# A hybrid decoder block in split fp32: the first unit's steps, the place of the units' joins, copies of operands, and a stored product added by transfer

## The chip, the cores and the metric

The kernel runs on one core of a Trainium2 chip. The metric is device microseconds of one execution. The time before is 2474.84 us, the median of three runs (2473.66 to 2476.01).

## The reference, cut to what matters

One layer on a sequence of 256 tokens with 4096 channels, all in fp32: a norm, one wide projection that gives seven parts, two branches (a pooling mixer and a short gated convolution, 2048 channels each), a merge by sigmoid gates, an output product with a residual, and a last norm.

```python
h = rmsnorm(x, norm_w[l])
proj = jnp.einsum('bsd,de->bse', h, w_in[l])
u_p, z_p, u_c, b_c, c_c, z_c, g_logit = jnp.split(proj, SPLIT_POINTS, axis=-1)
y_pool = causal_multiscale_pool(u_p, pool_w[l], pool_scale[l]) * jax.nn.silu(z_p)
y_conv = causal_gated_shortconv(u_c, b_c, c_c, conv_w[l], conv_b[l]) * jax.nn.silu(z_c)
ys = jnp.stack([y_pool, y_conv], axis=2)
br = jnp.einsum('bsnc,ncd->bsnd', ys, w_branch[l])
gates = jax.nn.sigmoid(g_logit.reshape(b, s, N_BRANCHES, d) + gate_b[l])
merged = jnp.sum(gates * br, axis=2)
x = x + jnp.einsum('bsd,de->bse', merged, w_out[l])
...
return rmsnorm(x, final_norm_w)
```

`causal_gated_shortconv` is `b_gate * (conv_b + taps over 3 tokens of (c_gate * u))`. `causal_multiscale_pool` is a trailing mean over 2, 4, 8 or 16 tokens less the token itself, times a 512 x 512 matrix for each of four groups.

## The kernel before, in words

**Split operands.** Each fp32 operand of a product is split into a high part (rounded to the type fp32r by ScalarE, `highs`, line 181) and a low part (the rest, by a subtraction on VectorE, `lows`, line 185). A product is three matmuls: high by high, high by low, low by high. Activations are the stationary operand (128 x 128, held split in `arena`), weights move (128 x 512, split in a ring of 15 cells, `ring`).

**Units.** The work is 32 units, each 256 tokens by 1024 output columns: for each half c of the convolution channels `cz`, `cb`, `cu`, `cc` (z, b, u and c parts of the projection); `pz`, `pu` for each half of the pooling channels; eight gate units `g0_c`, `g1_c`; eight branch units `b0_c` (pooling) and `b1_c` (convolution); four output units `o0` to `o3`. Their order is that of lines 702 to 714. A unit is a text of steps, one letter each; a step takes 256 input channels and a weight block of 1 MB (256 x 1024). **P** is a direct step: 8 products, 24 matmuls. **S** is a turned step: seven products in place of eight (21 matmuls), by the scheme of Strassen, with four sums of weight quarters on VectorE into the tile `parts` (lines 231 to 245) and four sums in the operand (`sums_s`, line 623). The x operands are 8 of kind P (4 blocks of 128 x 128, high and low) and 8 of kind S: six with 7 blocks and two with 8. An S operand of 8 blocks can also serve a direct step (`standing`, line 149). The first unit, cz0, has the text SIX5, `PPPPPSPSPSPSPSPS`; most others have EIGHT, `PSPSPSPSPSPSPSPS`; branch units have 8 steps (B0, B1).

**End of a unit.** Products collect in four PSUM banks E (direct sums) and, for S steps, four banks F (corners), which the transposes also use. When a bank has its last product, `evacuate` (line 341) copies an E bank by ScalarE into the tile E or Y, and `copy_corners` (line 347) an F bank into a slot of the raw ring, as soon as that slot (`Join`) has been given out. Behind the unit's last step `combine` (line 352) joins them on VectorE: two sums of 512, one subtraction of 1024, and two multiply-adds of 1024 by 1/rms (in the units of w_in) or one sum of 2048. Then the unit's epilogue is put on `queue`, from which each tick (six matmuls) pops one item (lines 888 to 893): `gap(n)` is n empty items. So `cb` has, after one empty item, E = E * Y (z times b), four empty ones and then 16 transposes in four items (line 386), whose results ScalarE copies into Y; a store to DRAM follows. `cc` does the same, with the taps of the convolution behind the transposes. `b0_c` multiplies by its gates (Y = E * Y) and stores the product to `p_d`; `b1_c` multiplies, loads `p_d` back into Y, adds it on VectorE ten items later, transposes and stores `m_d`.

**Preparation.** Weights come as 1 MB loads on SyncE's queue into a raw ring of three slots; a slot is loaded anew when its step has been prepared (`pump`, line 862). A deque `work` holds, step by step, the items that split the weights. An item is issued when its step is within `state["limit"]`, which `after_group` sets to four steps beyond the current one (line 918), and when ring cells are free. The order in which the program issues instructions is pinned, and each engine runs its own in that order. So on VectorE and ScalarE what stands ahead of a join is what `pump` had issued before `combine` is called. `issue_load` gives a unit's Join its raw slot after the first three loads of the next unit (line 831).

**x operands.** They are made during cz0. `xc` blocks come on SyncE's queue into the tile Y; `x_direct` makes a P operand (ScalarE scales by the norm weight, VectorE does the low part); for an S operand `x_scale`, `x_sums` and `x_rest` work through two staging tiles, sa and sa2, over three steps' items (lines 811 to 817). In the same unit the squares of x are taken (`fetch_rows`, `square`), and 1/rms from them (`root`, before step 14).

**y and m operands.** From the last gate unit (g1_3) on, regions of the arena whose x operand has been used for the last time are filled with y operands (from `y_d`), later with m operands (from `m_d`, or for the last four straight from Y, `fill_direct`). A `Fill` is fetched by a transfer on GpSimd's queue into sa or a second tile sb, and six ticks or more later `fill_staged` makes it: four sums on VectorE, a rounding on ScalarE, a subtraction on VectorE (`parts_of`, line 629).

**Lines that the profile names.** 52 is any ScalarE activation, 55 any two-input sum or product on VectorE, 67 a multiply-add, 70 a load on SyncE's queue, 73 and 76 a plain and an adding transfer on GpSimd's queue, 386 the transposes, 900 the products, 524 a copy in the band tables, 1029 the last scaling of the output.

## Time and profile before

| | |
|---|---|
| runs, median of three | 2474.84 us (2473.66 to 2476.01) |
| the profiled execution | 2475.68 us |
| its span in the profile | 2473.9 us |
| TensorE products / weight loads | 2390.4 us (97%) / 1964.9 us (79%), 10497 instructions each |
| VectorE | 2155.7 us (87%), 1769 instructions |
| ScalarE | 1445.6 us (58%), 1401 instructions |
| GpSimd | 86.3 us (3%) |
| bytes moved | 553.36 MB, mean 224 GB/s |

How to read it. The span runs from the first to the last record of the profile; the execution's own time is 1.8 us more. A busy share is a mean over the whole span and says little here, since TensorE's is 97% and matmuls are counted busy while they wait in its pipeline. What counts is the chain of work that ended last, what ends each of TensorE's idle times, and how long a unit takes beside the time that its matmuls need in a stretch without a wait. In a row of the trace the columns are the start in us, the busy time, the engine, the line, the operation with output and inputs, and in brackets the idle time of the engine just before with what ended it. In a table of windows each row is a stretch of the span, its length, TensorE's busy time with its instructions, the granted clock, the share of DMA and GB/s. VectorE is written DVE, ScalarE ACT, GpSimd POOL, SyncE SP.

### The profile page before, as it was taken

What the parts mean: (1) busy time and instruction counts of PE and PEld (TensorE: products, weight loads), DVE (VectorE), ACT (ScalarE), POOL (GpSimd) and SP (SyncE); (2) the same over time, 40 slices, a digit from 0 to 9 for tenths busy, and PEclk for the clock granted to TensorE, in tenths of its full rate; (3) what the DMA queues carried; (4) which work ended last, traced back from release to release, by engine and by line L of the source; (5) the groups of instructions that cost most, each with busy time, mean ns of one, the idle gap of its engine ahead of it and who ended that gap; (6) DMA issues with size and microseconds to landing.
All of it is one profiled execution on the core that took longest, in us unless ns stands there. A gap on an engine that the chain in (4) does not pass through costs nothing.

```text
span 2473.9 us, 26884 instructions
## 1 busy us (share of the span) xinstructions
PE 2390.4 (97%) x10497; PEld 1964.9 (79%) x10497; DVE 2155.7 (87%) x1769; ACT 1445.6 (58%) x1401; POOL 86.3 (3%) x150
## 2 busy tenths in 40 slices
PE   8898999998999999999999999999899999999998
PEld 7577887887878888888888888887688887778886
DVE  7897899888889878978988998888888888889998
ACT  6665555654655655655665666565565555566664
POOL 0000000000000000000000000001000001000000
PEclk9999999999999999999999999999999999999999
DMA  8464565555556555555765776577667767647667
GB/s 323 154 233 177 187 220 208 192 199 200 194 209 215 199 190 205 208 204 202 249 228 192 260 244 232 194 252 255 233 238 265 269 249 261 231 178 267 239 219 271
DMA packets 83215, 553.36 MB, mean 224 GB/s; under 512 B 9488, under 2 KB 9488, under 8 KB 21008
## 3 DMA queue, kind: packets, MB, share of 16 engines
q1 hardware_dynamic: 68832, 484.47, 54.0%
q0 software_dynamic: 13824, 66.07, 8.8%
q8 instruction: 82, 1.34, 0.2%
q10 hardware_dynamic: 432, 1.11, 0.1%
q14 instruction: 45, 0.37, 0.0%
HBM read 522.25 MB, written 29.36 MB: 223 GB/s over the span
## 4 chain that ended last, share of the span: by engine, by line
PE 82%; DVE 10%; ACT 4%; issue 2%; DMA 2%; SPq 0%; DVEq 0%; POOL 0%; ACTq 0%; POOLq 0%
PE sums L900 61%; PE shared L900 19%; DVE ring L55 4%; ACT ring L52 3%; DVE parts L55 2%; PE shared L560 1%; PE shared L386 1%; DVE raw L55 1%; DMA raw<-in_w_in_dram 1%; DVE E L55 1%; DVE sa L55 1%; DVE arena L55 1%; ACT raw L52 0%; DVE E L67 0%; ACT E L52 0%
## 5 line engine op out<-in xcount | busy, mean ns | idle before, releaser
L900 PE MATMUL sums<-ring,arena 128*128 128x512 f32 x7827 | 1841.1, 393 | 33.6 <-ACT E L52 14.3
L900 PEld LDWEIGHTS sums<-ring,arena 128*128 128x128 f32 x7827 | 1477.5, 189 | 351.9 <-DVE ring L55 18.8
L55 DVE TENSOR_TENSOR ring<-raw,ring 128x2048 fp32r<-128x2048 f32 (+3 forms) x518 | 935.0, 1815 | 190.9 <-ACT ring L52 190.2
L52 ACT ACTIVATE ring<-raw 128x2048 fp32r<-128x2048 f32 (+3 forms) x518 | 787.6, 1535 | 436.5 <-PE sums L900 264.3
L52 ACT ACTIVATE ring<-parts 128x1024 fp32r<-128x1024 f32 (+1 forms) x418 | 412.6, 1002 | 330.6 <-DVE parts L55 296.1
L900 PE MATMUL shared<-ring,arena 128*128 128x512 f32 x2340 | 568.9, 392 | 9.6 <-DVE ring L55 7.3
L900 PEld LDWEIGHTS shared<-ring,arena 128*128 128x128 f32 x2340 | 440.4, 189 | 106.2 <-DVE ring L55 11.7
L55 DVE TENSOR_TENSOR ring<-parts,ring 128x2048 fp32r<-128x2048 f32 (+3 forms) x233 | 449.2, 1940 | 55.6 <-ACT ring L52 55.0
L55 DVE TENSOR_TENSOR parts<-parts,raw 128x512 f32<-128x512 f32 x390 | 270.2, 693 | 13.3
L55 DVE TENSOR_TENSOR parts<-raw 128x1024 f32<-128x1024 f32 x195 | 238.0, 1221 | 3.8 <-DMA raw<-in_w_branch_dram 2.3
L55 DVE TENSOR_TENSOR raw<-raw 128x512 f32<-128x512 f32 (+1 forms) x93 | 80.6, 867 | 2.1
L52 ACT ACTIVATE raw<-shared 128x512 f32<-128x512 f32 x124 | 67.7, 610 | 7.8 <-DVE ring L55 7.3
L52 ACT ACTIVATE arena<-sa 128x512 fp32r<-128x512 f32 (+2 forms) x28 | 22.1, 790 | 73.2 <-DVE sa L55 69.3
L52 ACT ACTIVATE E<-sums,rin 128x512 f32<-128x512 f32 x56 | 36.0, 686 | 25.8 <-PE sums L900 25.8
L386 PE MATMUL shared<-ident,E 128*128 128x128 f32 x128 | 20.8, 301 | 25.9 <-DVE E L55 25.9
L386 PEld LDWEIGHTS shared<-ident,E 128*128 128x128 f32 x128 | 17.0, 156 | 30.8 <-issue 27.4
L67 DVE SCALAR_TENSOR_TENSOR E<-raw,rin,E 128x1024 f32<-128x1024 f32 x28 | 34.7, 1282 | 0.6
L55 DVE TENSOR_TENSOR E<-E,Y 128x2048 f32<-128x2048 f32 x15 | 34.3, 2286 | 0.1
L52 ACT ACTIVATE Y<-shared 128x512 f32<-128x512 f32 x24 | 13.4, 596 | 32.7 <-PE shared L386 30.2
L55 DVE TENSOR_TENSOR arena<-sa,arena 128x512 fp32r<-128x512 f32 (+2 forms) x28 | 24.9, 888 | 8.7 <-ACT arena L52 8.7
L52 ACT ACTIVATE E<-sums 128x512 f32<-128x512 f32 x44 | 25.1, 595 | 11.6 <-PE sums L900 10.4
L76 POOL DMA_DIRECT2D E<-in_rows_dram x16 | 13.9, 867 | 441.8 <-DVE E L67 439.6
(108 smaller groups left out, 428.5 us busy)
## 6 DMA issues: line engine op xcount, KB each, us to landing
raw<-in_w_in_dram SPq DMA_DIRECT2D x319, 1024.0 KB, 4.8
raw<-in_w_branch_dram SPq DMA_DIRECT2D x64, 1024.0 KB, 5.7
raw<-in_w_out_dram SPq DMA_DIRECT2D x64, 1024.0 KB, 4.9
E<-in_rows_dram POOLq DMA_DIRECT2D x16, 512.0 KB, 10.0
gates_d<-E POOLq DMA_DIRECT2D x8, 1024.0 KB, 6.6
Y<-gates_d POOLq DMA_DIRECT2D x8, 1024.0 KB, 6.5
Y<-in_xc_dram SPq DMA_DIRECT2D x16, 256.0 KB, 6.1
E<-in_x_dram POOLq DMA_DIRECT2D x4, 1024.0 KB, 6.4
```

Of the source, the lines that this page charges most:

```text
L52: return pin(nc.scalar.activation(dst, src, func, **kw))
L55: return pin(nc.vector.tensor_tensor(out=dst, in0=a, in1=b, op=op))
L67: return pin(nc.vector.scalar_tensor_tensor(out=dst, in0=a, scalar=s, in1=b, op0=op0, op1=op1, **kw))
L76: return pin(nc.gpsimd.dma_start(dst, src, accum_op=ALU.add))
L386: pin(nc.tensor.transpose(shared(j)[:, i * T + t * P:i * T + (t + 1) * P], src[:, t, c:c + P], ident))
L560: pin(nc.tensor.matmul(o, a, b, start=(k, i) == (0, 0), stop=(k, i) == (3, 2)))
L900: pin(nc.tensor.matmul(ps, lhs, rhs, start=n == 0, stop=n == u.total[b] - 1))
```

## The change

- **First unit.** cz0 gets an order of its own, `FIRST`, in which all 16 steps are direct. Operands 8 to 15 are the S operands; six of them have no eighth block, which a direct step needs, so a tile `extra` holds it while the opening's pool is open (now for the first 10 steps). sa2 is gone: all eight S operands are staged through sa, and the sums, high and low parts come in one item. The tile `parts` is allocated when the opening's pool closes. A unit without S steps gets no Join, and `combine` does no join for it.
- **Joins.** A unit may have an `urgent` function, called at the end of `combine`. `cb`, `cc` and `b1` have E = E * Y there, `b0` Y = E * Y and its store; `pu` has an empty one. For a unit that has one, `after_group` sets the limit of preparation, during its last step, to two steps beyond the current one in place of four. The empty items in the epilogues are adjusted, so that the transposes of cb and cc come after six, those of b1 after fifteen.
- **Copies.** High parts of S operands, of those filled directly and of the x operands too, are made by `tensor_copy` on VectorE. P operands keep ScalarE. `fill_direct` stages in sa.
- **p0.** In `b1` the load of `p_d` into Y and the sum on VectorE go; two adding transfers on GpSimd's queue, one for each half of the tokens (512 KB), add `p_d` to E.

```diff
+FIRST = (0, 8, 9, 1, 10, 11, 2, 12, 13, 3, 14, 15, 4, 5, 6, 7)
+OPENED = 10
...
-    sums = sb("parts", [P, 4, NH])
...
+    extra = op.tile([P, NS, 2, P], F32R, name="extra")
...
-            assert i < self.n
+            if i == self.n:
+                e = extra[:, self.region[1]]
+                return e[:, 0], e[:, 1]
...
     def combine(u):
         d = u.dst
-        copy_corners(u)
...
-        u.join.prepared = True
+        if u.s:
+            copy_corners(u)
...
+            u.join.prepared = True
         u.flags["base"] = True
+        if u.urgent:
+            u.urgent()
...
-            return gap(1) + [lambda: mul(E, E, Y)] + gap(4) + transposes(E, copy) + [lambda: move(g_d[c], Y)]
+            return gap(6) + transposes(E, copy) + [lambda: move(g_d[c], Y)]
...
-            items = gap(1) + [lambda: mul(E, E, Y)] + gap(4)
+            items = gap(6)
...
+        in_unit(f"cz{c}", base + 3 * HALF, lambda u: silu_y(), FIRST if first else SIX4, dst=Y)
+        in_unit(f"cb{c}", base + HALF, b_epi, EIGHT).urgent = lambda: mul(E, E, Y)
...
+        in_unit(f"cc{c}", base + 2 * HALF, c_epi, EIGHT).urgent = lambda: mul(E, E, Y)
...
+        in_unit(f"pu{c}", c * NU, lambda u: [], EIGHT).urgent = lambda: None
...
-                return gap(2) + [lambda: mul(Y, E, Y), lambda: move(p_d[c], Y)]
+                return []
...
-            return gap(1) + [lambda: mul(E, E, Y), lambda: move(Y, p_d[c])] + gap(9) + [
-                lambda: add(E, E, Y)] + gap(5) + pairs(transposes(E, copy)) + [
+            return gap(15) + pairs(transposes(E, copy)) + [
...
+        def urgent():
+            if n == 0:
+                mul(Y, E, Y)
+                move(p_d[c], Y)
+            else:
+                mul(E, E, Y)
+                for t in range(2):
+                    gather(E[:, t], p_d[c][:, t])
...
+    def copy(dst, src):
+        return pin(nc.vector.tensor_copy(dst, src))
+
     def fill_staged(o, st):
         if o.kind == "S":
             sums_s(st)
-            parts_of(o, st[:, 0:o.n])
+            copy(o.view[:, 0], st[:, 0:o.n])
+            sub(o.view[:, 1], st[:, 0:o.n], o.view[:, 0].bitcast(F32))
...
-                if part == 0:
-                    act(o.view[:, 0, lo:hi], q)
-                else:
-                    sub(o.view[:, 1, lo:hi], q, o.view[:, 0, lo:hi].bitcast(F32))
+            copy(o.view[:, 0, lo:hi], q)
+            sub(o.view[:, 1, lo:hi], q, o.view[:, 0, lo:hi].bitcast(F32))
...
     def x_sums(j):
-        o, st = x_ops[first_order[j]], x_stage(j)
-        sums_s(st)
-        act(o.view[:, 0], st[:, 0:o.n])
...
+        o = x_ops[first_order[j]]
+        fill_staged(o, sa)
+        if o.n == 7:
+            e = extra[:, o.region[1]]
+            copy(e[:, 0], sa[:, A21])
+            sub(e[:, 1], sa[:, A21], e[:, 0].bitcast(F32))
...
-            steps[j].mid.append(item(x_rest, j))
...
-        loaded += mine[:3] + ([units[v - 1].join] if v else []) + mine[3:]
+        loaded += mine[:3] + ([units[v - 1].join] if v and units[v - 1].s else []) + mine[3:]
...
         state["limit"] = state["now"] + min(AHEAD, state["now"] + 1)
+        if u.urgent and st is u.steps[-1]:
+            state["limit"] = state["now"] + 2
...
-        if u is units[1]:
-            opening.close()
...
+            if state["now"] == OPENED:
+                opening.close()
+                sums = ctx.enter_context(tc.tile_pool(name="parts", bufs=1)).tile([P, 4, NH], F32, name="parts")
```

More of the change, by code (lines that the diff above doesn't have):

```diff
@@ L311, in __init__ @@
             self.flags = {}
+            self.urgent = None
             self.pending = deque()
@@ L353, in combine @@
         d = u.dst
-        copy_corners(u)
-        assert not u.pending
-        q = u.join.slot
-        add(q[:, 0], q[:, 2], q[:, 0])
-        add(q[:, 3], q[:, 0], q[:, 3])
-        sub(q[:, 0:2], q[:, 1:2].to_broadcast([P, 2, NH]), q[:, 0::3])
-        q = q.rearrange("p (n t) c -> p t n c", n=2)
-        d4 = d.rearrange("p t (n c) -> p t n c", n=2)
-        if u.scaled:
-            for t in range(2):
-                stt(d4[:, t], q[:, t], rin[:, t:t + 1], d4[:, t], ALU.mult, ALU.add)
-        else:
-            add(d4, d4, q)
-        u.join.prepared = True
+        if u.s:
+            copy_corners(u)
+            assert not u.pending
+            q = u.join.slot
+            add(q[:, 0], q[:, 2], q[:, 0])
+            add(q[:, 3], q[:, 0], q[:, 3])
+            sub(q[:, 0:2], q[:, 1:2].to_broadcast([P, 2, NH]), q[:, 0::3])
+            q = q.rearrange("p (n t) c -> p t n c", n=2)
+            d4 = d.rearrange("p t (n c) -> p t n c", n=2)
+            if u.scaled:
+                for t in range(2):
+                    stt(d4[:, t], q[:, t], rin[:, t:t + 1], d4[:, t], ALU.mult, ALU.add)
+            else:
+                add(d4, d4, q)
+            u.join.prepared = True
         u.flags["base"] = True
+        if u.urgent:
+            u.urgent()
     def corners(d):
@@ L430, in seq_x @@
     def seq_x(text):
+        if text is FIRST:
+            return [("P", i) for i in FIRST]
         return sequence(text, ND, ND + NS + NB, NB)
@@ L599, in branch_unit @@
                  before=lambda: move(Y, gates_d[n, c]))
+        u.urgent = urgent
         units.append(u)
@@ L647, in fill_direct @@
         add(st[:, Q3], k1[:, 0], st[:, Q6])
-        for part in (0, 1):
-            for lo, hi, q in ((0, 4, st[:, 0:4]), (A12, A11, k1), (A11, o.n, k0[:, 0:o.n - A11])):
-                if part == 0:
-                    act(o.view[:, 0, lo:hi], q)
-                else:
-                    sub(o.view[:, 1, lo:hi], q, o.view[:, 0, lo:hi].bitcast(F32))
+        for lo, hi, q in ((0, 4, st[:, 0:4]), (A12, A11, k1), (A11, o.n, k0[:, 0:o.n - A11])):
+            copy(o.view[:, 0, lo:hi], q)
+            sub(o.view[:, 1, lo:hi], q, o.view[:, 0, lo:hi].bitcast(F32))
         o.ready = True
@@ L763, in square @@
         stt(q[:, 1], q[:, 1], 1.0, q[:, 1], ALU.mult, ALU.mult, accum_out=ssq[:, 1, c:c + 1])
-    first_order = [i for _, i in seq_x(SIX5)]
+    first_order = FIRST
     xt = Y.rearrange("p a n -> p (a n)").rearrange("p (s o c) -> p s o c", s=4, c=P)
```

25 lines of the change are left out of this document (8 added, 17 removed).

## The prediction

> **What bounds the kernel now.** I read the clock first, then the chain that ended last, then what TensorE waited for, then unit by unit how far TensorE is from its own pace.
>
> ```profile
> core 0: 2473.9 us, clock 0.985
> ```
> ```profile
> PE 82%; DVE 10%; ACT 4%; issue 2%; DMA 2%; SPq 0%; DVEq 0%; POOL 0%; ACTq 0%; POOLq 0%
> ```
> ```profile
> PE shared L386 <- DVE E L55: 25.9, 5, 8.0
> PE sums L900 <- ACT E L52: 14.3, 2, 10.2
> ```
>
> TensorE ends the chain for 82% of the span. Its waits are few and long: 25.9 us before transposes (line 386) for VectorE's product in E, and 14.3 us in two places for ScalarE's copy of finished sums. The pace comes from a stretch without a wait, the first row here; the second is the transposes' wait:
>
> ```profile
> 198.19 9.68 PE L900 MATMUL sums<-ring,arena 128*128 128x512 f32 x42
> 215.14 1.09 PE L386 MATMUL shared<-ident,E 128*128 128x128 f32 x4 [7.26 <-DVE E L55]
> ```
>
> 42 products take 9.68 us with the drain of the last one (about 0.4), so 0.227 us each: 5.44 a direct step (24), 4.76 an S step (21). At that pace a unit of 360, 363 or 366 products takes 81.7, 82.3 or 83.0 us. Against that stand the stretches of the units concerned (length, TensorE's busy time, granted clock): cz0, cb0, cu0, cz1, cu1, pz0, g1_3, b1_3, o0.
>
> ```profile
> 7.14:114.60 107.46, 93.59 (x366) 0.95 0.65 249
> 114.60:198.20 83.60, 82.08 (x362) 1.00 0.57 202
> 198.20:292.30 94.10, 86.84 (x381) 0.95 0.53 190
> 374.40:467.90 93.50, 87.84 (x383) 0.96 0.58 204
> 549.70:644.50 94.80, 86.84 (x381) 0.95 0.52 193
> 726.30:818.90 92.60, 87.72 (x383) 0.96 0.57 206
> 1671.50:1769.40 97.90, 85.37 (x367) 0.97 0.71 242
> 2070.90:2124.10 53.20, 44.34 (x184) 0.97 0.70 245
> 2124.10:2216.80 92.70, 88.72 (x383) 0.96 0.55 199
> ```
>
> Over the pace they stand by 24.5, 1.9, 11.8, 10.5, 12.5, 9.6, 14.9, 11.7 (of 41.5 for 183 products) and 9.7 us: 107 us in all, part of it a clock granted at half for some us after a wait (0.95 to 0.97). That is what the change can reach.
>
> **A. The first unit (cz0).** Six S steps become direct: 18 products more, +4.1 us of TensorE, and VectorE and ScalarE lose the six weight sums. But eight of the x operands are needed earlier, each with its sums on VectorE, through one buffer sa.
>
> The start is later. ScalarE's order puts the scaling of the second operand (in steps[0].pre) ahead of the rounding of the first weights.
>
> ```profile
> 7.54 1.06 ACT L52 ACTIVATE ring<-raw 128x1024 fp32r<-128x1024 f32 x1 [0.46 <-DMA raw<-in_w_in_dram]
> 9.69 0.91 ACT L52 ACTIVATE arena<-Y,par 128x256 fp32r<-128x256 f32 x2 [1.09 <-DMA Y<-in_xc_dram]
> ```
>
> The second operand lands at 9.7, its scaling ends at 10.6, the first rounded half is there at 11.7: the first product moves from 7.14 to 11.7. Then one S operand's share of VectorE:
>
> ```profile
> 26.99 2.29 DVE L55 TENSOR_TENSOR ring<-raw,ring 128x2048 fp32r<-128x2048 f32 x1 [1.52 <-ACT ring L52]
> 29.20 1.01 DVE L55 TENSOR_TENSOR sa<-sa 128x128 f32<-128x128 f32 x4
> ...
> 34.38 1.09 DVE L55 TENSOR_TENSOR arena<-sa,arena 128x896 fp32r<-128x896 f32 x1
> ```
> ```profile
> L524 DVE CAST bands<-sa x4: 211/215/215, 320.4 to 1037.5; 128x128 fp32r<-128x128 f32 x4
> ```
> ```profile
> L1029 DVE TENSOR_SCALAR raw<-raw,rout x4: 747/751/754, 2458.5 to 2466.0; 128x1024 f32<-128x1024 f32 x4
> ```
>
> The 896-wide copy is not in the trace. It lies between the 128-wide copy, 0.21, and the two-input subtraction of its own width, 1.09; on the line between the one-input rows (0.21 at 128, 0.75 at 1024) it is 0.67, which I take. An operand costs 1.01 + 0.67 + 1.09 + 0.5 for the extra block = 3.3 us. With one buffer the next scaling (0.9) waits for that, the rounding of the step's weights (two of 1.06) stands behind it on ScalarE, and VectorE's lows (2.29) behind that: 8.6 us for an S operand after an S operand, against 5.44 for the step. Two of three operands are of that kind. From 10.6: lows of step 0 until 14.0, operand 8 until 17.2, scaling and rounding until 20.1, lows until 22.3. So step 1 starts at about 22 (17.4 before). A round S, S, P then takes VectorE's chain 17.4 us, or 18.7 with a square, and TensorE 3 x 5.44 = 16.3. VectorE leads by about 2 us after each direct operand, so I count 2 us of waits: 22.3 + 15 x 5.44 + 2 = 106 for the end of cz0, 114.6 before. In cb0 VectorE's lag goes (83.60 less 82.08, 1.5 us). The start of cu0 moves from 198.2 to 188: **-10.5**. Bounds: -14 (no waits at all) and -3 (each copy at 1.09, the chain late from the first round on).
>
> **B. Four turns (cb0, cc0, cb1, cc1).** VectorE now runs the next units' S step ahead of the join:
>
> ```profile
> 203.22 1.22 DVE L55 TENSOR_TENSOR parts<-raw 128x1024 f32<-128x1024 f32 x1 [1.05 <-DMA raw<-in_w_in_dram]
> ...
> 207.48 2.67 DVE L55 TENSOR_TENSOR raw<-raw 128x512 f32<-128x512 f32 x3
> 210.19 2.48 DVE L67 SCALAR_TENSOR_TENSOR E<-raw,rin,E 128x1024 f32<-128x1024 f32 x2
> 212.70 2.29 DVE L55 TENSOR_TENSOR E<-E,Y 128x2048 f32<-128x2048 f32 x1
> ```
>
> ```profile
> 198.68 2.04 ACT L52 ACTIVATE ring<-raw 128x1024 fp32r<-128x1024 f32 x2
> 200.58 1.12 ACT L52 ACTIVATE raw<-shared 128x512 f32<-128x512 f32 x2
> ```
>
> The unit ended at T = 198.2, the join began 9.3 us later and took 7.5 with the product. Its last two corner copies stood behind a weight rounding and ended at 201.7. In the changed order only the lows of two steps, both done near T, are ahead of the join on VectorE, and the four corner copies (0.56 each) stand together on ScalarE, the last right after T: join from T+0.9, product done at T+8.4. TensorE asks for it after 42 products, T+9.5. So nothing waits. What is late next is the third step's lows: T+8.4 + 2.3 = T+10.7, needed at 48 products and one set of transposes, about T+11.5. Of the 44.4 us over the pace in these four units, 25.0 are the wait (25.9 less 0.9 in b0_3); I keep 2.4 each for 16 transposes, and the other 9.8 are the half clock after the wait (the clock column, 0.04 to 0.05 of each stretch, allows up to 17, part of it inside the wait). **-35**; bounds -37 and -17 (half the wait stays as a wait for lows).
>
> **C. Staged S operands on VectorE (g1_3 to b0_0).** ScalarE stands before an operand's rounding, with the finished sums behind it:
>
> ```profile
> 1767.85 0.95 ACT L52 ACTIVATE arena<-sb 128x896 fp32r<-128x896 f32 x1 [3.29 <-DVE sb L55]
> 1768.70 1.83 ACT L52 ACTIVATE E<-sums,rin 128x512 f32<-128x512 f32 x3
> ```
>
> That rounding goes to VectorE, where 0.67 takes the place of a wait of 1.02. The sums are then copied at about T+5.5, after a P operand's rounding (that stays on ScalarE) and a weight rounding: the wait of 10.2 becomes 5.5. With a little less lag before it: **-5.5** (bounds -9, -1).
>
> **D. b0 to b1, the new wait.** The product and the join now stand ahead of the third step's lows:
>
> ```profile
> 1814.31 2.29 DVE L55 TENSOR_TENSOR ring<-parts,ring 128x2048 fp32r<-128x2048 f32 x1 [2.06 <-ACT ring L52]
> ...
> 1819.34 2.67 DVE L55 TENSOR_TENSOR raw<-raw 128x512 f32<-128x512 f32 x3
> 1822.05 2.29 DVE L55 TENSOR_TENSOR E<-E,raw 128x2048 f32<-128x2048 f32 x1
> 1824.37 2.29 DVE L55 TENSOR_TENSOR Y<-E,Y 128x2048 f32<-128x2048 f32 x1
> ```
>
> ```profile
> 1813.62 6.96 PE L900 MATMUL sums<-ring,arena 128*128 128x512 f32 x30
> ```
>
> b1_0 begins at T = 1813.6. The S step's lows end at T+3.0, join +5.0, product +2.2, third lows +2.3: T+12.5. TensorE needs them after 45 products, T+10.3. Behind them stand the fourth step's lows, which then come in time. Three turns of 2.1: **+6.5** (bounds 0 and +13, if half clock follows each).
>
> A rule bears on that. The Trainium skill, "TensorE: Matmul & The Clock Gate", section "What's actually happening", has the clock fall to half only after an idle window of about 3.4 us; by it these waits cost 6.3 alone. The trace agrees in that cb0 kept 1.00 through a wait of 1.5.
>
> **E. p0 by adding transfers (b1 to b0, o0).** One load and one sum on VectorE (2.29, beside TensorE) go; two adding transfers of 512 KB come, as in the out units:
>
> ```profile
> DMA to landing us min/median/max: 7.8/10.2/12.6
> ```
>
> They are issued after the product: join from T+0.9, 5.0 long, product 2.2, T+8.2. The longest landing, 12.6, ends at T+20.8 and the time between the two issues; the transposes come after 16 ticks of 6 products, T+21.8. It fits by less than 1: **+1**; bounds 0 and +8 (2 us late in each of four). Behind them POOL holds the stores after the transposes and loads of operands that are needed a unit later.
>
> The Trainium skill, "SBUF — State Buffer", section "Who interferes with whom", says that VectorE copies in a two-port mode shut GpSimd out while they run, descriptor writing included. By it a transfer issued beside a staged copy lands up to 0.7 later, and the sum would be +2; no row here shows it.
>
> **F. b1_3 and o0.** ScalarE waits here too:
>
> ```profile
> 2085.34 0.95 ACT L52 ACTIVATE arena<-sa 128x896 fp32r<-128x896 f32 x1 [10.54 <-DVE sa L55]
> ```
>
> That goes, and with it the wait for sums at o0's start (4.0). But in b1_3 the third lows stand behind the S step's lows (T+3.0), an S operand (2.6), the join (5.0), the product (2.2) and a P operand's subtraction (0.6), and take 2.2: T+15.6, needed at T+10.3. That is a wait of 5.3 and 1.6 of half clock (now 0.97 of 53.2): 41.5 + 6.9 = 48.4, 53.2 before. In o0 the four direct fills, about 2.9 us each with their copies, stand ahead of the lows of steps 7 and 8: some 2.5 us of waits and 1 for E's late transfer, 89 (92.7). **-8.5** (bounds -13, -1).
>
> **Sum.** -10.5 - 35 - 5.5 + 6.5 + 1 - 8.5 = -52. The profiled execution took 2475.68 (span 2473.9 and 1.8 around it), 0.84 over the median of the three: 2475.7 - 52 = **2424**. All low ends give 2403, all high ends 2475.
>
> **Rivals.** (1) *The cap starves VectorE's lead, slower than before.* If the join can't begin at T+0.9 but only when it does now, T+9.3, the two-step cap keeps the third lows behind it until T+19: 7.5 us of new wait and 1.6 of clock at seven branch turns, +64 in the place of D's 6.5, and B's gain turned into +6: about 2522. To undo 52 us at eleven turns it takes 4.7 each, so it decides from a join at about T+6. For it: the join starts at T+9.3 now. Against it: all that stands ahead of it there is named in the rows of B, and is behind it in the new order. (2) *The opening gains nothing*: the 8.6 us chain holds every step; A is 0, 2434. (3) *The branch waits are larger*: each third step and each E some 3 us later with the clock's half, +20, 2444. (4) *The change does half of what it says at the turns*: VectorE arrives later than its order suggests, B is -17, 2442. (5) *Better*: no waits in D, A and F at their low ends, 2409.
>
> **How the numbers follow.** The forecast has 0.45; (5) 0.12, (2) 0.11, (3) 0.12, (4) 0.10, (1) 0.08; 0.02 for failures that add up to no change. All but (1) and those 0.02 end well below 2470, where 0.2% (5 us, about what a measurement of this kernel can tell from no change) begins: faster 0.90, same 0.02, slower 0.08. The range 2402 to 2452 holds these but for their tails, and leaves out about 0.18.
>
> **What would show it.** First product near 11.7, cz0's end near 106. The waits for E at line 386 fall from 25.9 to under 5, while waits of TensorE for ring appear at the third step of b1 units (2 each, 5 in b1_3). ScalarE shows no wait for sa or sb beyond the first unit's end. I am wrong if cu0 starts after 195, if the first row of waits stays above 12, or if the branch units b0_0 to b1_2 take over 320 us (now 1769.4 to 2070.9, 301.5; with D and E about 309).

## The result, and the profile after

The changed kernel takes 2464.19 us (median of five, 2460.64 to 2464.99) against 2476.01 us for the kernel before (median of five): a ratio of 0.9951, 95% interval 0.9937 to 0.9966. It is faster by 0.5%, about 12 us. The prediction was 2424, faster by 52.

The profiled execution took 2464.99 us, its span 2463.3, 10.6 less than before. The first views are of the same kinds as those before the change: span and clock, the chain that ended last, and TensorE's waits (total us, times, longest).

```profile
core 0: 2463.3 us, clock 0.989
```
```profile
PE 77%; DVE 12%; DMA 4%; ACT 4%; issue 3%; DVEq 0%; SPq 0%; ACTq 0%; POOL 0%; POOLq 0%
```
```profile
PE sums L913 <- DVE ring L57: 25.2, 15, 7.0
PE shared L913 <- DVE ring L57: 9.8, 4, 6.0
PE sums L913 <- ACT ring L54: 9.8, 3, 7.8
PE shared L913 <- DVE Y L69: 8.7, 4, 2.5
PE sums L913 <- ACT E L54: 4.5, 1, 4.5
...
PE shared L394 <- DVE E L57: 0.7, 2, 0.4
```

The line numbers have moved: 54 is ScalarE's activation, 57 VectorE's two-input operation, 69 its multiply-add, 72 SyncE's load, 75 and 78 GpSimd's transfers, 394 the transposes, 913 the products (in the experiments some differ by a few). The wait that the change aims at has gone: the transposes' wait for E fell from 25.9 us to 0.7. Two others stand in its place: products that wait for VectorE's weight parts (25.2 and 9.8 us), and products that wait for the convolution's taps (8.7, `DVE Y L69`). DMA has risen from 2% to 4% of the chain.

The stretches, as a table of windows (length, TensorE busy, then the other engines, the granted clock, DMA share, GB/s): cz0, cu0, cz1, cu1, pz0, g1_3, the seven units b0_0 to b0_3 (b1_0 to b1_2 among them), b1_3, o0.

```profile
12.87:108.40 95.53, 92.04 (x385) 74.49 (x386) 79.78 (x115) 53.21 (x64) 2.14 (x3) 0.98 0.74 276
...
190.00:274.10 84.10, 84.10 (x380) 69.69 (x379) 75.32 (x60) 50.09 (x50) 5.27 (x23) 1.00 0.60 217
356.10:448.50 92.40, 88.06 (x383) 71.39 (x381) 80.20 (x72) 49.94 (x52) 2.05 (x3) 0.96 0.58 206
530.30:614.90 84.60, 84.30 (x380) 69.61 (x379) 75.16 (x57) 50.14 (x48) 0.55 (x1) 1.00 0.58 212
696.50:788.90 92.40, 87.33 (x383) 71.02 (x382) 80.07 (x69) 49.64 (x50) 2.01 (x3) 0.98 0.57 206
1641.40:1733.80 92.40, 84.57 (x368) 68.18 (x366) 80.11 (x76) 52.51 (x52) 9.29 (x16) 1.00 0.71 240
1733.80:2052.30 318.50, 307.58 (x1341) 252.06 (x1342) 253.50 (x186) 170.42 (x172) 22.43 (x34) 0.98 0.71 248
2052.30:2107.20 54.90, 46.06 (x184) 37.04 (x183) 47.76 (x53) 26.41 (x31) 3.75 (x7) 0.91 0.67 237
2107.20:2206.00 98.80, 88.30 (x383) 71.60 (x383) 84.94 (x94) 46.98 (x45) 2.31 (x3) 0.97 0.55 187
```

The seven branch units took this before:

```profile
1769.40:2070.90 301.50, 300.95 (x1342) 248.95 (x1343) 258.02 (x184) 175.45 (x176) 18.63 (x31) 0.99 0.71 257
```

So the gain and the loss stand in different places. cu0 starts 8.2 us earlier than before (190.0 for 198.2); cu0 and cu1 take 84 for 94; g1_3 takes 92.4 for 97.9. But cz1 and pz0 hardly moved, the branch units lost 17, b1_3 and o0 together 7.8 (153.7 for 145.9).

**Why the branch units lost.** One turn shows it, from b1_1 to b0_2, at 1912.8. VectorE, on its timeline:

```profile
1914.12 2.68 DVE L57 TENSOR_TENSOR raw<-raw 128x512 f32<-128x512 f32 x3 [1.12 <-ACT raw L54]
1916.84 2.29 DVE L57 TENSOR_TENSOR E<-E,raw 128x2048 f32<-128x2048 f32 x1
1919.16 2.29 DVE L57 TENSOR_TENSOR E<-E,Y 128x2048 f32<-128x2048 f32 x1
1921.37 4.55 DVE L57 TENSOR_TENSOR ring<-raw,ring 128x2048 fp32r<-128x2048 f32 x3
1935.62 2.29 DVE L57 TENSOR_TENSOR ring<-raw,ring 128x2048 fp32r<-128x2048 f32 x1 [9.69 <-ACT ring L54]
```

Join and product run almost as early as predicted (1.3 to 8.6 us after the unit's end, 0.9 to 8.2 forecast). The lows of the third and fourth steps follow at once. But then VectorE stands idle for 9.7 us, waiting for ScalarE's rounding of the fifth step's weights, and ScalarE waits for the weights themselves:

```profile
1917.86 2.01 ACT L54 ACTIVATE ring<-raw 128x1536 fp32r<-128x1536 f32 x2 [1.96 <-DMA raw<-in_w_branch_dram]
1933.67 1.91 ACT L54 ACTIVATE ring<-raw 128x2048 fp32r<-128x2048 f32 x1 [13.80 <-DMA raw<-in_w_branch_dram]
```

There are three raw slots. A slot is free for the next load when VectorE has made its step's lows, or done the join in it. Here the lows of the third step stand behind join and product, so no weight load was issued between 1913.0 and 1923.7. SyncE's queue waited for VectorE, 10.6 us at the longest (total, times, longest; 1900 to 1942, and the same turn before the change, 1927 to 1969):

```profile
SPq L72 <- DVE ring L57: 30.3, 5, 10.6
```
```profile
SPq L70 <- DVE ring L55: 31.9, 7, 7.9
```

In all the queue waited no longer than before (there another 4.6 us were for the join). What is new is that one load goes out right after the turn and then none for 10.7 us, where before one went out every two to five (1940.9, 1945.1, 1950.0, 1952.2, 1956.6). Then three loads were issued within 2.3 us, the first of them 1.2 us behind the second adding transfer, and they landed 9.9 to 12.5 us later. TensorE was ready for the fifth step's lows at 1936.1 and had them at 1938.0. ScalarE's waits for weight loads in the seven branch units, after and then before, as the first row of each view:

```profile
ACT ring L54 <- DMA raw<-in_w_branch_dram: 106.3, 24, 13.8
```
```profile
ACT ring L52 <- DMA raw<-in_w_branch_dram: 37.5, 17, 4.3
```

**Why cz1 and pz0 gained nothing.** TensorE in cz1, which starts at 356.1:

```profile
375.48 6.40 PE L913 MATMUL sums<-ring,arena 128*128 128x512 f32 x27
381.71 0.84 PE L913 MATMUL shared<-ring,arena 128*128 128x512 f32 x3
384.54 2.24 PE L913 MATMUL shared<-ring,arena 128*128 128x512 f32 x6 [1.99 <-DVE Y L69]
388.56 1.62 PE L913 MATMUL shared<-ring,arena 128*128 128x512 f32 x3 [1.78 <-DVE Y L69]
```

The transposes no longer wait, but the fifth step is the first turned one, and its F banks are those of the transposes. They come free when VectorE has done the taps. VectorE, from 356.1: a join and product until 365.3, two steps' lows, 2.6 us of waiting for a load, a turned step's sums and lows, the next step's lows, and among them 16 taps of 0.47:

```profile
372.33 1.23 DVE L57 TENSOR_TENSOR parts<-raw 128x1024 f32<-128x1024 f32 x1 [2.57 <-DMA raw<-in_w_in_dram]
...
386.51 1.90 DVE L69 SCALAR_TENSOR_TENSOR Y<-shared,par,Y 128x255 f32<-128x255 f32 x4
```

The last tap ends at 388.4, 32 us after the unit's start. Before, the wait for E came first and hid this one.

### The profile page after: what moved, and what is told of

It reads as the page before. It is cut to its first block, busy times and chain, and to the rows that moved or that the text cites. A ratio compares the mean times of both kernels' runs of the same rounds, so it can differ in the third digit from the quotient of the medians.

```text
span 2463.3 us, 26875 instructions
## 1 busy us (share of the span) xinstructions
PE 2389.8 (97%) x10515; PEld 1966.2 (80%) x10515; DVE 2131.9 (87%) x1780; ACT 1410.6 (57%) x1358; POOL 91.8 (4%) x154
## 4 chain that ended last, share of the span: by engine, by line
PE 77%; DVE 12%; DMA 4%; ACT 4%; issue 3%; DVEq 0%; SPq 0%; ACTq 0%; POOL 0%; POOLq 0%
PE sums L913 57%; PE shared L913 18%; DVE ring L57 5%; DMA raw<-in_w_branch_dram 2%; ACT ring L54 2%; DVE parts L57 1%; DVE raw L57 1%; DVE E L57 1%; PE shared L570 1%; ACT raw L54 1%; ACT E L54 1%; DVE arena L57 1%; DMA raw<-in_w_in_dram 1%; DVE sa L57 0%; DVE Y L69 0%
## 5 line engine op out<-in xcount | busy, mean ns | idle before, releaser
L913 PE MATMUL sums<-ring,arena 128*128 128x512 f32 x7881 | 1850.7, 392 | 39.9 <-DVE ring L57 25.2
L54 ACT ACTIVATE ring<-parts 128x1024 fp32r<-128x1024 f32 (+1 forms) x402 | 399.7, 1009 | 360.2 <-DVE parts L57 323.0
L913 PE MATMUL shared<-ring,arena 128*128 128x512 f32 x2268 | 551.5, 392 | 18.5 <-DVE ring L57 9.8
L913 PEld LDWEIGHTS shared<-ring,arena 128*128 128x128 f32 x2268 | 426.5, 189 | 111.9 <-DVE ring L57 13.2
L57 DVE TENSOR_TENSOR ring<-parts,ring 128x2048 fp32r<-128x2048 f32 (+3 forms) x224 | 434.6, 1953 | 40.6 <-ACT ring L54 39.9
L57 DVE TENSOR_TENSOR parts<-parts,raw 128x512 f32<-128x512 f32 x378 | 262.0, 693 | 12.9
L69 DVE SCALAR_TENSOR_TENSOR E<-raw,rin,E 128x1024 f32<-128x1024 f32 x28 | 34.7, 1282 | 0.5
L57 DVE TENSOR_TENSOR E<-E,raw 128x2048 f32<-128x2048 f32 x11 | 25.2, 2292 | 0.4
L57 DVE TENSOR_TENSOR E<-E,Y 128x2048 f32<-128x2048 f32 x11 | 25.2, 2290 | 0.3
L570 PE MATMUL shared<-ring 128*128 128x512 f32 x96 | 22.1, 389 | 0.0
L570 PEld LDWEIGHTS shared<-ring 128*128 128x128 f32 x96 | 18.0, 188 | 3.7
```

Of the source, the lines that this page charges most:

```text
L54: return pin(nc.scalar.activation(dst, src, func, **kw))
L57: return pin(nc.vector.tensor_tensor(out=dst, in0=a, in1=b, op=op))
L69: return pin(nc.vector.scalar_tensor_tensor(out=dst, in0=a, scalar=s, in1=b, op0=op0, op1=op1, **kw))
L570: pin(nc.tensor.matmul(o, a, b, start=(k, i) == (0, 0), stop=(k, i) == (3, 2)))
L913: pin(nc.tensor.matmul(ps, lhs, rhs, start=n == 0, stop=n == u.total[b] - 1))
```

## The experiments

The theory is called "lead given up": VectorE's lead over TensorE, up to four prepared steps, is what it can spend at a turn. The change spends it to have the join early, and the raw slots, which are freed by VectorE, pass the delay on to the loads. Times are of single executions, except for the last one; lengths of units are from the profiles. The five executions of the changed kernel lie 4 us apart, so where two times differ by less than that, the lengths of units decide. One source of such differences is the opening: with the same code there, the first product started at 11.5 to 11.8 us in five of the runs (the first four experiments and e8) and at 12.8 to 12.9 in four (the changed kernel, e5, e7 and e9), as the second operand landed.

**e1_branch_old**: no urgent function in b0 and b1, so also no limit of two steps there, and p0 by a load and a sum as before the change.

```diff
-                return []
+                return gap(2) + [lambda: mul(Y, E, Y), lambda: move(p_d[c], Y)]
...
-            return gap(15) + pairs(transposes(E, copy)) + [
+            return gap(1) + [lambda: mul(E, E, Y), lambda: move(Y, p_d[c])] + gap(9) + [
+                lambda: add(E, E, Y)] + gap(5) + pairs(transposes(E, copy)) + [
...
-        u.urgent = urgent
```

> The changed kernel with the branch units as they were: no urgent function and no limit of two in b0 and b1, the product in the epilogue, p0 loaded and added on VectorE. Theory 'lead given up': in the changed kernel join and product stand ahead of the lows of the third step at every branch turn, the raw slots behind them are freed late, so the loads are issued late; the stretch b0_0 to b1_2 (318.5 us changed, 301.5 before), b1_3 (54.9) and o0 (98.8) all suffer from that. Then here b0_0 to b1_2 takes 301 to 303, b1_3 about 48, o0 about 90: some 2432 to 2438. Rival 'copies': the 6.4 us wait in o0 and the 7.4 us wait in b1_3 are VectorE's own new work in the fills. Then o0 stays at 96 or more and b1_3 at 53 or more: 2444 to 2448.

Measured 2431.4 us. The branch units, b1_3 and o0:

```profile
1732.60:2033.40 300.80, 300.57 (x1342) 248.74 (x1343) 262.03 (x190) 174.05 (x174) 18.63 (x31) 0.99 0.72 263
2033.40:2080.00 46.60, 43.62 (x184) 35.32 (x183) 43.45 (x46) 25.05 (x28) 3.77 (x7) 0.96 0.83 276
2080.00:2172.50 92.50, 86.73 (x384) 71.22 (x384) 89.16 (x99) 47.44 (x45) 1.06 (x2) 0.98 0.55 203
```

300.8 for 318.5, 46.6 for 54.9, 92.5 for 98.8: this part of the change had cost 32 us. The copies on VectorE, still there, are not the cause of the waits in b1_3 and most of o0, though VectorE does more work here than in the changed kernel (262 for 253.5). o0 fell a little less than forecast.

**e2_load_add**: p0 by a load and a sum, the urgent product kept.

```diff
-            return gap(15) + pairs(transposes(E, copy)) + [
+            return gap(10) + [lambda: add(E, E, Y)] + gap(5) + pairs(transposes(E, copy)) + [
...
-                for t in range(2):
-                    gather(E[:, t], p_d[c][:, t])
+                move(Y, p_d[c])
```

> The changed kernel with one thing undone: p0 comes by a load into Y right behind the urgent product and a sum on VectorE ten items later, in place of two adding transfers. The same bytes move at the same time. Theory 'lead given up': the waits at the fifth step of b0_1, b0_2, b0_3 (1.1, 2.3, 2.3 us, with half clock behind) come from weight loads that are issued 10 us late; they stay, 2462 to 2466. Rival 'adding transfers': such a transfer holds the DMA engines longer than a load of the same bytes, and the three weight loads issued beside it (9.9 us to landing, 4.8 otherwise) come late for that; then b0_1 to b0_3 fall from 140.8 to about 133, 2456.

Measured 2470.2, slower than either theory had it. The fifth step's wait, which the theory had stay, went, so the adding transfers did have a part in it: at the same turn the three loads beside the plain transfer landed after 6.1 to 8.8 us, beside the adding ones after 9.9 to 12.5. But the sum stands on VectorE behind that late work, and TensorE's transposes wait for it:

```profile
PE shared L394 <- DVE E L57: 15.0, 3, 5.6
PE sums L912 <- DVE ring L57: 5.7, 3, 1.9
```

So an adding transfer is the lesser evil once the lead is gone.

**e3_no_cap**: the limit of two steps taken out, the product still right behind the join.

```diff
-        if u.urgent and st is u.steps[-1]:
-            state["limit"] = state["now"] + 2
```

> The changed kernel without the limit of two steps; the urgent product stays behind the join. Theory 'lead given up': with four steps prepared ahead of the join, the waits for lows at the third step of the b1 units (2.3 to 2.6, 7.4 in b1_3) and at the fifth of the b0 units go, b0_0 to b1_2 takes about 303, and the waits for E come back: cu0 and cu1 at 93 (now 84.2, 84.7). 2464 - 15 - 6 + 18 = about 2461. Rival: the product's place right behind the join does the work in cu0 and cu1, and they stay at 84 to 86: about 2443.

Measured 2456.0. cu0, the branch units and o0:

```profile
188.70:282.30 93.60, 86.12 (x380) 71.01 (x379) 75.94 (x60) 50.66 (x50) 5.62 (x23) 0.96 0.54 195
...
1746.90:2053.50 306.60, 302.06 (x1341) 249.34 (x1342) 256.15 (x187) 174.08 (x174) 22.46 (x34) 0.99 0.75 261
...
2099.20:2196.90 97.70, 89.76 (x384) 73.46 (x383) 86.39 (x95) 49.10 (x47) 2.30 (x3) 0.95 0.54 189
```

The limit is what gives cu0 and cu1 their 10 us each (93.6 without it, 84.1 with it), and what costs the branch units about 12 (306.6, 318.5). The urgent product alone does nothing for cu0. What is left in the branch units, 306.6 for 300.8, are transposes that wait for an adding transfer, 4.5 us in three places. The product's early place costs them nothing by itself: e9, where it is late, has 306.6 too. In b1_3 the limit costs 9.2 (45.7, 54.9), but in o0 only 1.1 (97.7, 98.8).

**e4_five_direct**: cz1 and pz0 with one direct step more ahead of the first turned one.

```diff
-        in_unit(f"cz{c}", base + 3 * HALF, lambda u: silu_y(), FIRST if first else SIX4, dst=Y)
+        in_unit(f"cz{c}", base + 3 * HALF, lambda u: silu_y(), FIRST if first else SIX5, dst=Y)
...
-                HOST if c else SIX4, dst=Y)
+                HOST if c else SIX5, dst=Y)
```

> The changed kernel with the text of cz1 and pz0 changed to five direct steps before the first turned one (PPPPPSPS... in place of PPPPSPSP...): as many steps of each kind, the first turned step one step (5.44 us) later. Theory 'taps': the gain of the turns into cz1 and pz0 (92.4 us each, 9.4 over the pace) is eaten by F banks, which the first turned step needs while VectorE still owes them the convolution's taps behind join, lows and weight sums: 27 us of VectorE work plus 4.5 of waits for a load, from the unit's start, against 24 us of TensorE. One step more of TensorE (5.44) against 2.3 more of VectorE: cz1 and pz0 fall to 85 to 88, in all 2452 to 2457. Rival: the taps wait for TensorE's transposes and their ticks alone, and the banks come free late whatever stands before; then the wait moves with the step and 92 stays, 2463.

Measured 2455.9. cz1 and pz0 take 88.3 and 88.8 for 92.4, no more work done or saved: the order of steps alone. In cz1 two waits of 0.5 are left there, one for weights and one for the taps.

```profile
355.00:443.30 88.30, 86.39 (x383) 69.79 (x382) 79.39 (x70) 49.40 (x50) 2.06 (x3) 1.00 0.60 215
691.20:780.00 88.80, 87.12 (x383) 71.18 (x383) 79.30 (x69) 49.44 (x50) 2.02 (x3) 0.98 0.59 215
```

**e5_copies_on_scalar**: on top of e1, S operands' high parts back on ScalarE, for y and m.

```diff
-            copy(o.view[:, 0], st[:, 0:o.n])
+            (act if o in late else copy)(o.view[:, 0], st[:, 0:o.n])
...
-            copy(o.view[:, 0, lo:hi], q)
+            act(o.view[:, 0, lo:hi], q)
...
+    late = set(y_ops[0] + y_ops[1] + m_ops)
```

> e1_branch_old (2431.4 us) with the high parts of the y and m operands of kind S back on ScalarE, as in the kernel before; the x operands' copies stay on VectorE. Theory 'ScalarE's queue': g1_3 and b0_0 (together 136.1 in e1) go back to about 142, since finished sums stand behind a rounding that waits for VectorE, and b1_3 and o0 together (139.1) to 142 to 145: 2440 in all. Rival: the gain there came from somewhere else (the limit, the opening), and the copies are only moved: 2430 to 2433.

Measured 2446.7, 15 slower than e1. g1_3 with b0_0 takes 144.6 (136.1 in e1), b1_3 53.1 (46.6), o0 93.0 (92.5). The copies on VectorE are worth that much, and in b1_3 more than I had said.

**e6_weights_first**: on top of e1, the second x operand scaled behind the first weights' rounding.

```diff
-            steps[j - 1].pre.append(item(x_scale, j))
+            (steps[j - 1].mid if j == 1 else steps[j - 1].pre).append(item(x_scale, j))
```

> e1_branch_old with one item moved: the scaling of the second x operand stands behind the first step's weights on ScalarE, not ahead of them. Theory 'ScalarE's order': the first product starts at about 8 instead of 12.9 us, and the second step, which waits for VectorE's chain of operand and lows, starts at 18 to 20 instead of 21.3; from there TensorE sets the pace, so cz0 ends 2 to 3 us earlier, 2429. Rival: the chain on VectorE (lows, operand, lows) sets the second step's start whatever the order on ScalarE: the same time, 2431.

Measured 2429.6; the lengths show more than the time. The first product starts at 7.0 us in place of 11.8 in e1, and cz0 ends at 105.4 in place of 107.2. The order on ScalarE costs the changed opening 1.8 us; the other 3 go to VectorE's chain, which sets the second step's start. In the three later kernels with this edit cz0 ends at 103.8 to 105.1, without it nowhere before 107.0.

**e7_limit_three**: on top of e1, the limit at three steps.

```diff
-            state["limit"] = state["now"] + 2
+            state["limit"] = state["now"] + 3
```

> e1_branch_old with the limit at three steps beyond the current one in place of two, in the units that have one (cb, cc, pu). Theory 'lead given up': the limit trades the time of the join against the lead. With one step more ahead of the join (2.3 or 6.8 us of VectorE) the product of cb and cc comes at 11 to 15 us after the unit's end instead of 8.4, TensorE asks for it at 9.5: cu0 and cu1 rise from 84.2 and 84.7 to 86 to 90, while cz1 and pz0 (92.4, where the lead is missing at the fifth step) stay or fall by 2: 2431 to 2440. Rival: the limit matters only for what is loaded, and the join waits for the corner copies anyway: no change, 2431.

Measured 2435.9. cu0 88.5 and cu1 87.7 (84.2 and 84.7 in e1), cz1 90.4 and pz0 89.6 (92.4 and 92.3). One step of lead costs cu0 and cu1 4.3 and 3.0 us and gives cz1 and pz0 2.0 and 2.7 back, as the theory says. Of these, the 2.0 in cz1 is little more than its lengths differ by with the same code (92.4 in e1, 90.8 in e5 and e9).

**e8_five_direct_spread**: on top of e1, the texts of e4, the same text for g1_3, and direct fills at least nine ticks apart.

```diff
-                if f.ready():
+                if f.ready() and (force or now[0] >= spaced[0]):
+                    spaced[0] = now[0] + 9
...
-        text = HOST if (n, c) == (0, 0) else SIX4 if (n, c) == (1, 3) else EIGHT
+        text = HOST if (n, c) == (0, 0) else SIX5 if (n, c) == (1, 3) else EIGHT
```

> e1_branch_old with three edits that theory 'lead given up' suggests: cz1 and pz0 with five direct steps first (as in e4), g1_3 with the same text (it then ends on a turned step, whose E banks close 12 products before the end, so that ScalarE has their copies done when b0_0 starts), and the four direct fills in o0 at least nine ticks (54 products) apart instead of back to back. cz1 and pz0 to 88.5 each (-7.7), the start of b0_0 without its 4.9 wait (-4), o0 without the 5.0 wait at its tenth step (-5): about 2415. Rival 'VectorE's total': in g1_3 and o0 VectorE is behind by its whole work and not by its order, and waits of the same sum come back elsewhere in these units: about 2424.

Measured 2420.3, between theory and rival. o0 took 86.4 (92.5): the four fills, back to back on VectorE, had been what stood ahead of the tenth step's lows. g1_3 fell to 87.1, but b0_0 rose to 49.3 (43.8), where ScalarE stood for a late transfer of a y operand:

```profile
1745.41 0.63 ACT L54 ACTIVATE arena<-sa 128x512 fp32r<-128x512 f32 x1 [5.18 <-DMA sa<-y_d]
```

**e9_adding_alone**: on top of e1, p0 by adding transfers, the product left in the epilogue.

```diff
-            return gap(1) + [lambda: mul(E, E, Y), lambda: move(Y, p_d[c])] + gap(9) + [
-                lambda: add(E, E, Y)] + gap(5) + pairs(transposes(E, copy)) + [
+            def other():
+                for t in range(2):
+                    gather(E[:, t], p_d[c][:, t])
+            return gap(1) + [lambda: mul(E, E, Y), other] + gap(15) + pairs(transposes(E, copy)) + [
```

> e1_branch_old (2431.4 us) with the one part of the change at the branch units that it had left out and that makes nobody wait: in b1 the product stays in the epilogue, but p0 comes by two adding transfers behind it instead of a load and a sum. Theory 'lead given up': the losses of the changed kernel in b0 and b1 come from join and product being ahead of the third step's lows, not from the adding transfers; here b0_1 to b1_2 stay at 44.0 and 41.5, and 2.3 us of VectorE go at each b1 turn, among them the wait of 1.6 for E in o0: 2429 to 2432. Rival 'the adding transfers hold the DMA engines': b0_1 to b0_3 rise to 46 or more: 2438.

Measured 2440.1, 8.7 slower than e1: I was wrong that they make nobody wait. The branch units take 306.6 (300.8) and o0 96.0 (92.5), with this wait:

```profile
PE shared L394 <- DMA E<-p_d: 6.1, 4, 2.6
```

The second of the two adding transfers landed 11.6 to 12.4 us after its issue, and the room for it behind a product that comes late is less than that. In the changed kernel, where the product comes early, it took 10.3 to 11.9 and nobody waited. The rival's sum was about right (2438), its mechanism only in part: TensorE waits for the transfer itself and not for weights behind it.

**e10_five_late_fills**: e8 with e6's edit and `LANDING` at 10 in place of 6.

```diff
-    LANDING, STORED = 6, 7
+    LANDING, STORED = 10, 7
```

> e8_five_direct_spread (2420.3 us) with the first step's weights rounded ahead of the second operand's scaling (as in e6) and with the y and m fills taken up ten ticks after their fetch in place of six. In e8's b0_0 ScalarE and then VectorE stand for 3 to 5 us at a fill whose transfer is late (15.7 us to landing beside the gate unit's adding transfers), and TensorE waits 4.7 for it. Theory: that wait goes with the later fill: b0_0 from 49.3 to 43 to 45, with the opening's 1.8 about 2413 to 2415. Rival: VectorE or the loads are late there anyway and the wait comes back at another step of b0_0 or b1_0: 2418.

Measured 2416.6. b0_0 fell to 42.2 and g1_3 to 83.0, the pace itself, but b1_0 rose to 49.7 (43.2 in e8) and o0 to 92.3: late fills pile up and are paid for later. The time lies between the theory (2413 to 2415) and the rival (2418), and the wait came back elsewhere, as the rival has it.

**e11_six_late_fills**: as e10, with a text `PPPPPPSPSPSPSPSS` in cz1 and pz0 and g1_3 as it was.

```diff
+SIX6 = "PPPPPPSPSPSPSPSS"
...
-        in_unit(f"cz{c}", base + 3 * HALF, lambda u: silu_y(), FIRST if first else SIX5, dst=Y)
+        in_unit(f"cz{c}", base + 3 * HALF, lambda u: silu_y(), FIRST if first else SIX6, dst=Y)
```

> As e10, but cz1 and pz0 have six direct steps first (PPPPPPSPSPSPSPSS) and g1_3 has its old text (four direct steps first, a direct step last). Theory 'lead given up': with one more direct step VectorE's lead at the first turned step grows by another 3.1 us, and the waits left in cz1 and pz0 (2.3 each, beside 2.4 for the 16 transposes) go: 86 each, -5; g1_3 with b0_0 at 134 to 136 by the later fills. About 2411 to 2414. Rival: the two turned steps at the unit's end take the lead away there (2 x 6.75 us of VectorE against 2 x 4.76 of TensorE) and the wait moves to cb1 and pu0: 2416 to 2420.

Measured 2410.2. cz1 and pz0 take 85.5 and 85.6, that is 2.5 over the pace, most of it the 16 transposes. cb1 and pu0 stay at 81.6 and 81.7: the waits for the taps are gone without coming back. g1_3 with b0_0 took 127.5, well below the 134 to 136 expected, and part of that was lost in b1_0 (47.5, 43.2 in e8).

**e12_combined**: e11 with ten ticks for the y fills alone, `LANDING` being 6 again.

```diff
-            elif f.at is not None and (force or now[0] >= f.at + LANDING):
+            elif f.at is not None and (force or now[0] >= f.at + LANDING + 4 * (f.o in SLOW)):
...
+    SLOW = set(y_ops[0] + y_ops[1])
```

> As e11_six_late_fills (2410.2 us), but only the y fills are taken up ten ticks after their fetch, the m fills six ticks after it as before. In e11 o0 took 92.5 us, with a wait of 5.2 for E, and 86.4 in e8, where the m fills came after six ticks; b1_3 took 43.9 in e11 and 46.7 in e8. Theory: late m fills pile up on VectorE ahead of the product and the sum that o0's transposes need; o0 returns to 86 to 87 and b1_3 to 46.7, -3 in all: 2406 to 2409, about 67 us below the kernel before (2475). Rival: the later y fills have shifted the m fills already, o0 stays at 92: 2410 to 2413.

Measured 2408.75 us (median of five, 2408.15 to 2410.57) against 2476.16: a ratio of 0.973, interval 0.9716 to 0.9743. It is faster than both kernels. That it is faster than e11 isn't shown by the time, since e11's single 2410.2 lies inside the range of these five; o0 fell by 5 as expected, but b1_3 rose by 2.8 (43.9 to 46.7), expected too. cz1, pz0, the branch units and o0:

```profile
352.70:438.20 85.50, 85.10 (x384) 70.20 (x384) 78.14 (x69) 49.14 (x49) 2.05 (x3) 1.00 0.60 221
686.10:771.60 85.50, 85.17 (x383) 70.09 (x382) 78.15 (x70) 49.01 (x51) 2.02 (x3) 1.00 0.61 222
1709.50:2013.80 304.30, 300.82 (x1341) 248.71 (x1342) 266.00 (x199) 175.21 (x176) 20.81 (x35) 0.99 0.72 262
2060.50:2148.00 87.50, 85.58 (x383) 70.12 (x382) 86.13 (x97) 45.44 (x43) 1.06 (x2) 1.00 0.59 213
```

## Why the prediction was wrong, point by point

| term | predicted | measured, from the lengths of units |
|---|---|---|
| A, opening | -10.5 | -8.2 (start of cu0) |
| B, four conv turns | -35 | -21.5 (cu0 -9.9, cz1 -1.2, cu1 -10.1, pz0 -0.3) |
| C, g1_3 to b0_0 | -5.5 | -5.9 (142.1 to 136.2) |
| D and E, b1_0 to b0_3 | +7.5 | +17.5 (257.3 to 274.8) |
| F, b1_3 and o0 | -8.5 | +7.8 (145.9 to 153.7) |

The measured terms add up to -10.3, the spans differ by 10.6. Of the 42 us missed, F is 16, B 13.5, D and E 10, A 2.3, and C gives 0.4 back.

- **A** was right in its mechanism and 2.3 short in size. The first product came at 12.9 (11.7 forecast), since the second operand landed at 10.9, not 9.7. The 896-wide copy took 0.63 (0.67 taken). TensorE's wait in the second step ended at 23.6 (22 forecast), and cz0 at 108.4 (106). About 1.2 of this is the landing, which falls one way or the other from run to run: in e1, with the same opening, the first product came at 11.8 and cu0 began at 188.8. The rest is waits in later steps, and 0.3 that were summed wrong: 198.2 less 188 is 10.2.
- **B** was right at half of the turns: the product was done 9.2 us after the turn to cu0 (8.4 forecast), still before TensorE asked for it at 9.5, and cu0 and cu1 stand 1.9 and 2.4 over the pace. Its step "What is late next is the third step's lows" failed for cz1 and pz0. There the F banks are next, held by taps that stand behind that very work. I had looked at the first 48 products after the turn and not at the first step that needs an F bank. e4 and e11 show it by the order of steps alone. (The wait in b0_3 that B takes off is 0.5, not 0.9; that changes nothing.)
- **C** held, and e5 confirms it.
- **D** was right in place and size for the third step: waits of 1.9 to 2.2 at the third step of b1_0 to b1_2, 2.1 forecast. These three units grew by 9.5 in all (6.5 forecast), the other three, b0_1 to b0_3, by 8.1, which nothing in D had. "Behind them stand the fourth step's lows, which then come in time" is true of the fourth, and the failure is that I stopped there. The fifth step's load waits for a slot that those lows free. I had traced what is queued behind the wait on VectorE, and not the loads on SyncE's queue that wait for VectorE.
- **E** counted only whether E is there in time, and it was. That transfers beside the weight loads make these land later was left out. Two things count. Loads issued 4 us apart behind adding transfers landed after 9.2 to 11.3 us (e9, the turns into b0_1 to b0_3), at the same places behind the plain transfer after 6.2 to 7.4 (e1): some 2 to 4 us for the adding transfers. Where three loads went out together, the third took about 3 us longer than the first, beside adding transfers (changed kernel) and beside a plain one (e2).
- **F** is in b1_3 the same miss with less room. b1_3 waited 7.0 at the third step where 5.3 was forecast; the granted clock then was 0.91 over the unit. o0 had the ten idle microseconds on VectorE that b0_2 shows, and then three of the four direct fills ahead of the eighth step's lows, where TensorE waited 6.0 and 2.5 had been forecast for the fills. Here the miss is E's more than the limit's: o0 takes 98.8, without the limit still 97.7 (e3), and with the adding transfers alone 96.0 for 92.5 (e9, e1).
- Rival (1), the cap that starves VectorE's lead, had the right mechanism and the wrong trigger. I let it hang on a late join and gave it 0.08. It needs no late join: the limit itself takes the lead, in the branch units and at half of B.
- The clock. The Trainium skill, "TensorE: Matmul & The Clock Gate", section "What's actually happening", has the clock fall only after an idle window of about 3.4 us, and by that the waits of D would have cost themselves alone. Three windows of the changed kernel, each from the end of a wait, show otherwise, and the measurement decides: after 2.2 us in b1_1 the granted clock was 0.60 for the next 4.3, after 1.8 us in b0_2 0.57 for the next 4.0, after 1.9 us in b1_2 it was 1.00. So the length of the wait alone doesn't settle it; the last section says what does.

```profile
1880.10:1884.40 4.30, 4.30 (x12) 3.39 (x13) 2.08 (x1) 0.00 (x0) 0.53 (x1) 0.60 1.01 345
1938.00:1942.00 4.00, 4.00 (x15) 3.42 (x16) 3.93 (x4) 2.47 (x3) 0.00 (x0) 0.57 0.72 252
1973.30:1977.30 4.00, 4.00 (x18) 3.30 (x19) 2.12 (x1) 0.00 (x0) 0.54 (x1) 1.00 0.99 338
```

## What to carry to other kernels

Work that is pulled ahead of an engine's prepared lead spends that lead, and what the lead had hidden comes next: follow the engine's queue past the first consumer, to the first step that needs each shared buffer (here PSUM banks) and to every load that waits for a buffer that the engine frees. Pull forward only where somebody waits for the result: at two of the conv turns it gave 10 us each, at the branch turns, where nobody waited, it and the adding transfers cost 32 us in all. Where a lead is short, an order of steps that puts the cheap ones for that engine first can give it back for nothing.

## What the runs showed of the hardware that was not expected

- A wait of 2.2 or 1.8 us can halve TensorE's granted clock, for 3.4 us in these two cases, and one of 1.9 us can leave it at full speed (rows above). In each of the 14 traces the stretches at half clock begin on a grid of 3.41 us. What decides, as far as these traces show, is TensorE's busy share, as the profile has it, in the 3.41 us of the grid just before. From 16.5 us on and starting at full clock, the clock fell after 87 of 88 such windows with a share under 0.45, after 8 of 31 with 0.45 to 0.53, and after none of the 9649 above that. The window up to 1880.36, for one, had 1.19 us of work in 3.41 (0.35), and half clock followed.
- 1 MB loads issued beside two adding transfers of 512 KB landed after 9.9 to 12.5 us, beside one plain transfer of the same 1 MB after 6.1 to 8.8 us (the turn into b0_2, in the changed kernel and in e2). Over all four such turns it was 9.5 to 13.5 against 5.8 to 10.2.
